# A diffusion layer on one core: modulation weights in a ring of half tiles, the latent rows loaded through another queue

## The chip, the cores and the metric

The kernel runs on one core of one Trainium2 chip. The metric is device time in microseconds (us) for one execution of the whole layer. The engines are named as the profile names them: PE (matrix products) with PEld (its weight loads), DVE (vector), ACT (scalar functions), POOL (GpSimd), and SP, which here issues most of the DMAs. Each engine runs its own instructions strictly in order. A DMA is issued from the instruction queue of SP or POOL, so an issue that has to wait for a free buffer holds up whatever stands behind it on that queue.

## The reference, cut to what matters

```
m       = silu(cond) @ w_mod + b_mod            # 6 vectors: shift, scale, gate for two norms; 2 conditions
h       = rms_norm(x) * g * (1 + scale1) + shift1
q,k,v,xr,yg = split(h @ w_in)
o       = concat(window_attention(q,k,v,sink), rglru(conv(xr)) * gelu(yg)) @ w_out
x1      = x + gate1 * o
h2      = rms_norm(x1) * g * (1 + scale2) + shift2
y       = x1 + gate2 * PEER(h2)                 # 8 heads, top 16 of 128x128 product keys, 16384 experts
out     = rms_norm(y) * g_final
```

There are 256 context tokens, which read only context, and 1024 latent tokens, which read their window and all the context keys; the latent recurrence starts from given states. All of it is float32. A product of two float32 matrices is done as three products of their high and low parts.

## The kernel before

A tile is 128 tokens: there are 2 context tiles and 8 latent ones. The stages, with the names that the profile's rows carry:

1. **Modulation** (`modulations`, L156). `w_mod` is 24 MB, in 3 parts of 8 blocks. Each block is one DMA of 1 MB into a tile `w` of 8 KB per partition, in a ring of 6 (48 KB per partition), and feeds 4 products (L190) that add into a PSUM tile `p`, of which there are two. Part 0 gives `a1` and `b1`, the scale and shift of the first norm. The function then yields; parts 1 and 2, of use from the output projection on, are written after the context attention but may be placed anywhere earlier.
2. **Context first norm and projection** (`project`, L258). For each tile: sum of squares on ACT (L277), `rstd_of` (a power on POOL, L147, small DVE steps), scaling on DVE (L279), 8 transposes on PE (L248) whose results DVE (L253) and ACT (L255) scale and shift, and a split into high and low parts `hh` (ACT, L134) and `hl` (DVE, L135). Then 14 column blocks of `w_in` (load L286, split `wh` on ACT, `wl` on DVE, 24 products each), with the recurrence `recur` between them.
3. **Context attention**, scores L424, exponentials L439; **context finish** (`finish`, `w_out` loads L501, products L526); **context choice** of experts (`choose`, `combine`).
4. **Latent**: the same `project`, with the rows of `x_sample` loaded by SP (L272) into two buffers `x`, with two buffers `f`; then recurrence, rotary turns on POOL (L333), attention, finish, choice.
5. **Spread** (L697 to L709): one-hot products that write the weights of the chosen experts as a dense matrix for 6 latent tiles. Early experts (products `u`, L1028) run beside it. **Dense** experts from about 1703 us to the end.
6. **Gathers**: the other 4 tiles (2 context, 2 latent) fetch each chosen expert's two rows by indirect DMAs on POOL (L859 for `peer_u`, L873 for `peer_v`), one DVE instruction each (L862, L879). They are 4 x 128 rows of either kind. A counter (`tick`) issues them a few at a time between the other work, from the context choice on; those of the context tiles are 512 DVE instructions with their gathers, the first 249 of which stand ahead of the dense stage.

What sets the order: a list scheduler takes the instructions by priority (the order in which they are written, with `tick`'s insertions) as soon as its own model finds the inputs ready and a buffer free, and so fixes the order on each engine before the program runs. SBUF pools are stacked from either end. A pool that opens after others have closed takes their addresses and then has to wait for their last readers. The latent first norm's `x` and `f` tiles lay on addresses of the modulation pool and so came after the last L190.

## Time and profile before

| | |
|---|---|
| median of 3 runs | 3565.87 us (3563.97 to 3566.43) |
| profiled execution | 3568.34 us |
| its span | 3566.5 us |
| mean granted clock of PE | 0.955 of full speed |
| busy: PE, DVE, ACT, POOL | 90%, 87%, 40%, 48% of the span |
| chain that ended last | PE 43%, DVE 22%, issue 8%, DMA 8% |

The shares of busy time are means over stages that have different limits. The rows further down therefore cut the span into ten stretches, whose borders are: 41.5 us, the first split `wh` of the context projection; 128.9 us, the first exponential of the context attention; 173.4 us, its last output; 252.2 us, the context choice; 482.6 us, the first rotary product; 690 us, the latent finish; 885 us, the latent choice; 1230 us, the spread; 1619.4 us, the last product of the spread; 1703 us, the dense stage. An engine whose busy time nearly fills a stretch limits it there; where none does, a chain of waits or a DMA does.

### The profile page before, as it was taken

To read this page: it belongs to the slowest core of one execution; us is meant where nothing else is said; L and a number is where in the kernel's file an instruction comes from. 1 tells how busy PE (TensorE), PEld (TensorE's weight loads), DVE (VectorE), ACT (ScalarE), POOL (GpSimd) and SP (SyncE) were. 2 spreads that over 40 slices of the span, in tenths; PEclk is the share of its full clock that TensorE was granted. 3 is DMA by queue.
4 is the path that set the end of the run, shared out by engine and by line. 5 is a ranking of instruction groups with operands and counts; after the bars stand their busy time and mean duration, and the time that the engine had idled before them with its cause. 6 is when DMAs were issued, how large, how long until landed. Compare 5 with 4: busy or idle time off the path is not lost.

```text
span 3566.5 us, 48580 instructions
## 1 busy us (share of the span) xinstructions
PE 3210.4 (90%) x16982; PEld 2704.1 (76%) x16982; DVE 3111.0 (87%) x6762; ACT 1429.9 (40%) x2242; POOL 1716.4 (48%) x1146
## 2 busy tenths in 40 slices
PE   7788868777999888888899999999999999999994
PEld 4477645433889877778788888878888887888884
DVE  4649989877999999993599999989999998999998
ACT  5734647523112344433333334333334333333432
POOL 0012451466521223443266666656666655666665
PEclk9799989988999999999999999999999999999997
DMA  8342652588621367795699999989999998999996
GB/s 331 136 152 82 216 206 83 185 276 290 219 89 31 122 199 214 233 315 185 242 325 337 337 330 334 340 308 335 329 328 339 327 340 290 332 327 336 335 339 223
DMA packets 349141, 918.19 MB, mean 257 GB/s; under 512 B 29144, under 2 KB 150104, under 8 KB 345824
## 3 DMA queue, kind: packets, MB, share of 16 engines
q0 software_dynamic: 147456, 536.94, 42.9%
q1 hardware_dynamic: 201440, 378.16, 30.8%
q8 instruction: 133, 2.18, 0.2%
q14 instruction: 112, 0.92, 0.1%
HBM read 834.48 MB, written 80.50 MB: 257 GB/s over the span
## 4 chain that ended last, share of the span: by engine, by line
PE 43%; DVE 22%; issue 8%; DMA 8%; POOL 3%; ACT 2%; SPq 0%; POOLq 0%; DVEq 0%; ACTq 0%
PE u L138 6%; PE u L140 6%; PE u L139 6%; PE rot L138 5%; PE rot L140 5%; PE rot L139 5%; DVE acc L879 3%; DVE row L862 3%; DMA row<-in_peer_u,eid 2%; PE res L138 2%; PE res L139 2%; PE res L140 2%; DMA row<-in_peer_v,eid 2%; DMA ad<-a 2%; DVE oh L699 1%
## 5 line engine op out<-in xcount | busy, mean ns | idle before, releaser
L859 POOL DMA_INDIRECT row<-in_peer_u,eid x512 | 749.9, 1465 | 603.3 <-DVE acc L879 201.7
L873 POOL DMA_INDIRECT row<-in_peer_v,eid x512 | 719.9, 1406 | 583.6 <-DVE acc L879 283.7
L138 PE MATMUL u<-hh,uh 128*128 128x384 f32 x2048 | 707.1, 345 | 22.4 <-ACT a L1028 22.4
L140 PE MATMUL u<-hh,ul 128*128 128x384 f32 x2048 | 705.6, 345 | 4.7 <-DVE ul L135 4.7
L139 PE MATMUL u<-hl,uh 128*128 128x384 f32 x2048 | 707.1, 345 | 0.0
L879 DVE SCALAR_TENSOR_TENSOR acc<-row,w,acc 128x1024 f32<-128x1024 f32 x508 | 663.4, 1306 | 25.2 <-DMA row<-in_peer_v,eid 23.7
L862 DVE SCALAR_TENSOR_TENSOR row<-row,h 128x1024 f32<-128x1024 f32 x512 | 623.0, 1232 | 62.8 <-DMA row<-in_peer_u,eid 62.6
L764 ACT ACTIVATE q<-rot 128x512 f32<-128x512 f32 x504 | 300.0, 597 | 523.5 <-PE rot L140 295.5
L138 PE MATMUL rot<-vh,ah 128*128 128x512 f32 x1024 | 409.1, 400 | 16.6 <-ACT q L764 16.1
L138 PEld LDWEIGHTS u<-hh,uh 128*128 128x128 f32 x2048 | 394.7, 193 | 29.8 <-ACT a L1028 23.8
L140 PEld LDWEIGHTS u<-hh,ul 128*128 128x128 f32 x2048 | 394.2, 192 | 9.7 <-DVE ul L135 5.1
L139 PE MATMUL rot<-vl,ah 128*128 128x512 f32 x1024 | 401.4, 392 | 0.0
L140 PE MATMUL rot<-vh,al 128*128 128x512 f32 x1024 | 400.6, 392 | 0.0
L139 PEld LDWEIGHTS u<-hl,uh 128*128 128x128 f32 x2048 | 394.6, 193 | 4.5
L765 DVE TENSOR_TENSOR acc<-q,acc 128x512 f32<-128x512 f32 x504 | 341.8, 686 | 45.4 <-ACT q L764 42.3
L140 PE MATMUL mm<-hh,wl 128*128 128x256 f32 (+2 forms) x848 | 289.7, 342 | 9.8 <-POOL wl L135 6.9
L138 PE MATMUL mm<-hh,wh 128*128 128x256 f32 (+2 forms) x848 | 286.3, 338 | 5.6 <-ACT wh L134 5.6
L139 PE MATMUL mm<-hl,wh 128*128 128x256 f32 (+2 forms) x848 | 284.3, 335 | 0.0
L134 ACT ACTIVATE uh<-u 128x1024 fp32r<-128x1024 f32 x128 | 135.8, 1061 | 331.3 <-PE u L139 302.0
L135 POOL TENSOR_TENSOR ul<-u,uh 128x1024 fp32r<-128x1024 f32 x44 | 122.8, 2791 | 277.8 <-ACT uh L134 237.5
L138 PEld LDWEIGHTS rot<-vh,ah 128*128 128x128 f32 x1024 | 193.4, 189 | 74.9 <-ACT q L764 36.7
L140 PEld LDWEIGHTS rot<-vh,al 128*128 128x128 f32 x1024 | 193.2, 189 | 41.5
(271 smaller groups left out, 5955.3 us busy)
## 6 DMA issues: line engine op xcount, KB each, us to landing
u<-in_ut SPq DMA_DIRECT2D x128, 512.0 KB
v<-in_peer_v SPq DMA_DIRECT2D x128, 512.0 KB
gd<-stg SPq DMA_DIRECT2D x12, 4096.0 KB
gt<-gd SPq DMA_DIRECT2D x64, 768.0 KB
w<-in_w_mod SPq DMA_DIRECT2D x24, 1024.0 KB
ad<-a SPq DMA_DIRECT2D x88, 192.0 KB
a<-ad SPq DMA_DIRECT2D x44, 384.0 KB
w<-in_w_query SPq DMA_DIRECT2D x32, 512.0 KB
```

The lines of the kernel that those rows point to most:

```text
L134: A.activation(hi, src, AF.Copy)
L135: return (eng or V).tensor_tensor(lo, src, hi, op=OP.subtract)
L138: T.matmul(out, lhs[0], rhs[0], start=first, stop=False)
L139: T.matmul(out, lhs[0], rhs[1], start=False, stop=False)
L140: T.matmul(out, lhs[1], rhs[0], start=False, stop=last)
L699: V.tensor_tensor(oh.rearrange(four, j=2), o2.rearrange(four, j=2), pairs(gh, ts), op=OP.mult)
L764: A.activation(q, p, AF.Copy)
L765: tick(share / (2 * (N_DENSE - N_RES)), V.tensor_tensor(y, q, y, op=OP.add))
L859: G.indirect_dma_start(out=u, out_offset=None, in_=i["peer_u"], in_offset=bass.IndirectOffsetOnAxis(ap=eid[:, k:k + 1], axis=0))
L862: V.scalar_tensor_tensor(u, u, 1.0, h2, op0=OP.mult, op1=OP.mult, accum_out=act[:, j:j + 1])
L873: G.indirect_dma_start(out=v, out_offset=None, in_=i["peer_v"], in_offset=bass.IndirectOffsetOnAxis(ap=eid[:, k:k + 1], axis=0))
L879: V.scalar_tensor_tensor(acc, v, w[:, j:j + 1], acc, op0=OP.mult, op1=OP.add)
```

## The change

One PSUM tile `p` instead of two. Each block of `w_mod` comes as two DMAs of 0.5 MB into tiles of 4 KB per partition, in a ring of 4 such halves (16 KB per partition). The latent first norm's pool is no longer stacked on the modulation pool. Its rows are loaded from POOL's queue. Lines after L179 are numbered one higher in the changed kernel.

```diff
--- before.py
+++ after.py
@@ -173,10 +173,11 @@
         bmod = p1.tile([P, 3, 512], F32, name="bmod")
         modr = p1.tile([P, 3, 512], F32, name="modr")
         for n in range(3):
-            p = ps.tile([P, 512], F32, name="p", bufs=2)
+            p = ps.tile([P, 512], F32, name="p")
             for k in range(KD):
-                w = p1.tile([P, 4, 512], F32, name="w", bufs=6)
-                nc.sync.dma_start(w, i["w_mod"][n, k])
+                ws = [p1.tile([P, 2, 512], F32, name="w", bufs=4) for _ in range(2)]
+                for h, w in enumerate(ws):
+                    nc.sync.dma_start(w, i["w_mod"][n, k, :, 2 * h:2 * h + 2])
                 if n == 0 and k in (2, 3):
                     u = len(xc)
                     xc.append(p1.tile([P, D], F32, name=f"x{u}"))
@@ -187,7 +188,7 @@
                     gffn = load("gffn", [P, KD])
                     nc.sync.dma_start(bmod, i["bmod"])
                 for j in range(4):
-                    T.matmul(p[32 * j:32 * j + 32], sig[:, k], w[:, j], start=(k == 0), stop=(k == KD - 1),
+                    T.matmul(p[32 * j:32 * j + 32], sig[:, k], ws[j // 2][:, j % 2], start=(k == 0), stop=(k == KD - 1),
                              tile_position=(0, 32 * j), skip_group_check=True)
             V.tensor_tensor(modr[:, n], p, bmod[:, n], op=OP.add)
             pc = ps.tile([P, 4, P], F32, name="pc")
@@ -269,7 +270,7 @@
                 us = slice(u * P, (u + 1) * P)
                 if lat:
                     x = xp.tile([P, D], F32, name="x", bufs=2)
-                    nc.sync.dma_start(x, x_in[us, :])
+                    G.dma_start(x, x_in[us, :])
                 else:
                     x = xc[u]
                 f = xp.tile([P, KD, P], F32, name="f", bufs=2)
```

The scheduler's order changes with it up to the start of the dense stage; from there on the order is the same on every engine. Three places:

**SP from the context attention to the context finish.** `x_sample` are the latent rows, `w_out` the weights of the output projection, `w_in` here those of the latent input projection. Before:

```order
L272 DMA x<-in_x_sample 128x1024 x2
L319 DMA out_new_k<-kk 128x2x128
L207 DMA modd<-modr 2x512 x2
L272 DMA x<-in_x_sample 128x1024
L929 DMA out_new_rnn<-ends 128x8
L350 DMA wg<-in_w_rg 128x256 x2
L272 DMA x<-in_x_sample 128x1024 x5
L501 DMA w<-in_w_out 128x256 x8
```

After:

```order
L320 DMA out_new_k<-kk 128x2x128
L208 DMA modd<-modr 2x512 x2
L930 DMA out_new_rnn<-ends 128x8
L351 DMA wg<-in_w_rg 128x256 x2
L287 DMA w<-in_w_in 128x1024 x3
L502 DMA w<-in_w_out 128x256 x8
L212 DMA ga_1422<-modd 128x1024
L518 DMA x<-in_x_prompt 128x1024 x2
L287 DMA w<-in_w_in 128x1024
```

The eight loads of latent rows have left SP's queue. The first `w_out` loads stood behind five of them; now three latent `w_in` loads stand ahead. All eight row loads are now on POOL's queue, two at its very start and six between the powers L147.

**ACT at the start of the context attention.** `f<-tr` and `hh` belong to the latent first norm, `f,ss` is its sum of squares, `pr` are the exponentials. Before:

```order
L255 ACTIVATE f<-tr,b_89,a_88 128x128
L370 ACT_TABLE_LOAD
L370 ACTIVATE bv_877<-bv_877 128x256
L439 ACT_TABLE_LOAD
L439 ACTIVATE pr,sums<-s,negm 128x256 x2
L255 ACTIVATE f<-tr,b_89,a_88 128x128 x2
L134 ACTIVATE hh<-f 128x8x128
L439 ACTIVATE pr,sums<-s,negm 128x256 x2
L443 ACTIVATE den<-den 128x4
L277 ACTIVATE f,ss<-x 128x1024
L450 ACTIVATE pr<-pr,den 128x256 x4
L439 ACTIVATE pr,sums<-s,negm 128x256 x2
```

After:

```order
L256 ACTIVATE f<-tr,b_89,a_88 128x128
L371 ACT_TABLE_LOAD
L371 ACTIVATE bv_893<-bv_893 128x256
L440 ACT_TABLE_LOAD
L440 ACTIVATE pr,sums<-s,negm 128x256 x2
L256 ACTIVATE f<-tr,b_89,a_88 128x128
L134 ACTIVATE hh<-f 128x8x128
L440 ACTIVATE pr,sums<-s,negm 128x256 x2
L444 ACTIVATE den<-den 128x4
L451 ACTIVATE pr<-pr,den 128x256 x4
L440 ACTIVATE pr,sums<-s,negm 128x256 x2
L470 ACTIVATE pT<-pt 128x512
```

The norm of the latent tiles stood among the exponentials. It now stands ahead of them: three of its sums of squares and four of its transposes' copies come before the first `wh` of the context projection, and between that and the first exponential ACT has 5 sums of squares (2 before), 11 L255 (1) and 6 `hh` (0).

**POOL and DVE where the gathers stand.** On POOL, from the last power of the norm to the first rotary products `kT` and `qT`. Before:

```order
L147 TENSOR_TENSOR rs_r<-rs_m,nhalf 128x1 x12
L135 TENSOR_TENSOR wl<-w,wh 128x1024 x16
L859 DMA row<-in_peer_u,eid_2156 128x1024 x16
L873 DMA row<-in_peer_v,eid_2156 128x1024 x16
L859 DMA row<-in_peer_u,eid_2156 128x1024 x11
L333 TENSOR_TENSOR kT<-kT,cosT 128x512
L859 DMA row<-in_peer_u,eid_2156 128x1024
L333 TENSOR_TENSOR kT<-kT,cosT 128x512
L333 TENSOR_TENSOR qT<-qT,cosT 128x512 x6
```

After:

```order
L147 TENSOR_TENSOR rs_r<-rs_m,nhalf 128x1 x4
L135 TENSOR_TENSOR wl<-w,wh 128x1024 x16
L860 DMA row<-in_peer_u,eid_2204 128x1024 x16
L874 DMA row<-in_peer_v,eid_2204 128x1024 x16
L860 DMA row<-in_peer_u,eid_2204 128x1024 x16
L874 DMA row<-in_peer_v,eid_2204 128x1024 x7
L334 TENSOR_TENSOR kT<-kT,cosT 128x512
L874 DMA row<-in_peer_v,eid_2204 128x1024
L334 TENSOR_TENSOR kT<-kT,cosT 128x512
L334 TENSOR_TENSOR qT<-qT,cosT 128x512 x6
```

Sixteen `peer_u` gathers and then sixteen `peer_v` gathers make a block. 55 gathers are issued ahead of the first rotary product where there were 43; 12 more DVE row instructions (52, were 40) stand ahead of it too. Counted the same way, the number of row instructions done before a point rises by 16 at the first latent score, 18 at the last, 18 at the first latent norm of the finish, 23 at the last split there, 22 at the last choice and 26 at the first step of the spread, and is the same, 249, after the last step: 39 stood within the spread, now 13.

On DVE at the end of the spread (`oh` are its one-hot matrices; L613, L614 after the change, begins the last `combine`). Before:

```order
L697 TENSOR_TENSOR oh_13001<-iota,tw_12615 128x1024
L700 TENSOR_TENSOR oh_12977<-oh_12977,tw_12618 128x1024
L698 TENSOR_TENSOR oh_13002<-iota,tw_12616 128x1024
L879 SCALAR_TENSOR_TENSOR acc<-row,w,acc 128x1024
L699 TENSOR_TENSOR oh_13003<-oh_13002,tw_12617 128x1024
L613 TENSOR_TENSOR key<-idxs_6676 128x4x16
L700 TENSOR_TENSOR oh_13002<-oh_13002,tw_12618 128x1024
L613 TENSOR_TENSOR cand<-vals_6675 128x4x8
```

After:

```order
L701 TENSOR_TENSOR oh_13000<-oh_13000,tw_12666 128x1024
L699 TENSOR_TENSOR oh_13025<-iota,tw_12664 128x1024
L700 TENSOR_TENSOR oh_13026<-oh_13025,tw_12665 128x1024
L698 TENSOR_TENSOR oh_13049<-iota,tw_12663 128x1024
L701 TENSOR_TENSOR oh_13025<-oh_13025,tw_12666 128x1024
L699 TENSOR_TENSOR oh_13050<-iota,tw_12664 128x1024
L700 TENSOR_TENSOR oh_13051<-oh_13050,tw_12665 128x1024
L701 TENSOR_TENSOR oh_13050<-oh_13050,tw_12666 128x1024
L135 TENSOR_TENSOR vl<-v,vh 128x1024
```

The last `combine` came after the spread's last one-hot matrices; it now ends among them. On PE the early experts' products `u` within the spread fall from 1220 to 1152, 48 of them being one step of an early expert.

## Rows read from the trace of the kernel before

**Rows 1.** Stretches: length, busy us of PE, PEld, DVE, ACT, POOL, clock, DMA, GB/s

```profile
0.00:41.50 41.50, 21.06 (x108) 5.94 (x108) 13.09 (x56) 9.32 (x17) 1.29 (x6) 0.92 0.95 368
41.50:128.90 87.40, 75.19 (x500) 55.12 (x500) 48.81 (x99) 69.13 (x103) 1.60 (x2) 0.95 0.71 257
128.90:173.40 44.50, 33.86 (x112) 18.50 (x112) 32.06 (x102) 33.78 (x88) 2.70 (x5) 0.65 0.20 58
173.40:252.20 78.80, 67.38 (x306) 53.09 (x307) 29.73 (x58) 31.15 (x53) 6.53 (x6) 0.96 0.49 158
252.20:482.60 230.40, 202.60 (x996) 157.67 (x994) 211.09 (x729) 128.20 (x164) 95.98 (x56) 0.98 0.49 159
482.60:690.00 207.40, 157.07 (x863) 99.01 (x865) 180.36 (x361) 121.31 (x268) 67.29 (x56) 0.90 0.41 134
690.00:885.00 195.00, 141.49 (x389) 67.00 (x387) 138.39 (x200) 58.97 (x113) 121.58 (x96) 0.87 0.84 284
885.00:1230.00 345.00, 313.65 (x1882) 302.13 (x1881) 335.85 (x1972) 81.28 (x133) 108.51 (x68) 0.94 0.38 120
1230.00:1619.40 389.40, 341.50 (x2783) 301.39 (x2781) 368.32 (x801) 169.66 (x206) 134.74 (x64) 0.95 0.76 233
1619.40:1703.00 83.60, 73.81 (x417) 73.17 (x414) 24.69 (x166) 22.88 (x34) 21.51 (x12) 0.96 0.50 160
```

**Rows 2.** DMA packets in 63-67, 15-20 and 155-162 us

```profile
DMA packets 221, 1.68 MB, mean 420 GB/s; under 512 B 16, under 2 KB 16, under 8 KB 16
...
DMA packets 352, 2.09 MB, mean 418 GB/s; under 512 B 33, under 2 KB 33, under 8 KB 161
...
DMA packets 144, 0.52 MB, mean 75 GB/s; under 512 B 16, under 2 KB 16, under 8 KB 144
q1 hardware_dynamic: 144, 0.52, 23.1%
```

**Rows 3.** SP's issues in order: start, length, line, tensor, count

```profile
29.28 1.33 SPq L179 DMA_DIRECT2D w<-in_w_mod  x3
30.66 1.49 SPq L286 DMA_DIRECT2D w<-in_w_in  x2
...
132.70 38.95 SPq L272 DMA_DIRECT2D x<-in_x_sample  x5
```

**Rows 4.** PE in order: start, length, line, count, idle before and releaser

```profile
34.19 1.97 PE L248 MATMUL tr<-ident,x 128*128 128x128 f32 x8 [2.31 <-ACT f L255]
42.61 0.39 PE L138 MATMUL mm<-hh,wh 128*128 128x256 f32 x1 [1.71 <-ACT wh L134]
```

**Rows 5.** ACT by line and shape, 103-203 us: busy, mean ns | idle

```profile
L134 ACT ACTIVATE hh<-f 128x1024 fp32r<-128x1024 f32 x8 | 8.4, 1055 | 0.1
L277 ACT ACTIVATE f<-x 128x1024 f32<-128x1024 f32 x8 | 8.4, 1053 | 4.7 <-DVE hl L135 4.7
L255 ACT ACTIVATE f<-tr,b,a 128x128 f32<-128x128 f32 x16 | 7.1, 456 | 21.1 <-DVE f L253 20.4 <-DVE ends L382 0.7
```

**Rows 6.** DVE by line and shape, 253 to 482 us

```profile
L371 DVE SCALAR_TENSOR_TENSOR gi<-gi,xc 128x1024 f32<-128x1024 f32 x8 | 9.8, 1220 | 0.2 <-ACT gi L359 0.2
L375 DVE TENSOR_TENSOR_SCAN bv<-av,chan,gi 128x1024 f32<-128x1024 f32 x4 | 9.4, 2346 | 0.0
```

**Rows 7.** DVE by line, 690 to 885 us: busy, mean ns | idle, releaser

```profile
L879 DVE SCALAR_TENSOR_TENSOR acc<-row,w,acc 128x1024 f32<-128x1024 f32 x44 | 56.5, 1284 | 22.1 <-DMA row<-in_peer_v,eid 21.4
L862 DVE SCALAR_TENSOR_TENSOR row<-row,h 128x1024 f32<-128x1024 f32 x42 | 53.0, 1269 | 27.4 <-DMA row<-in_peer_u,eid 27.2
```

**Rows 8.** The same, 1230 to 1620 us, the spread

```profile
L879 DVE SCALAR_TENSOR_TENSOR acc<-row,w,acc 128x1024 f32<-128x1024 f32 x23 | 35.6, 1547 | 0.0
L862 DVE SCALAR_TENSOR_TENSOR row<-row,h 128x1024 f32<-128x1024 f32 x16 | 21.6, 1351 | 0.0
```

**Rows 9.** The columns of rows 1, while the last choice is combined

```profile
1616.40:1640.00 23.60, 16.73 (x107) 16.10 (x105) 21.82 (x133) 10.39 (x14) 6.75 (x4) 0.96 0.91 276
```

**Rows 10.** ACT in order of time: start, length, line [idle, releaser]

```profile
1636.64 1.28 ACT L627 ACT_TABLE_LOAD   x1 [9.05 <-DVE nm L626]
```

## Prediction

> **What bounds the kernel now.** I read the busy time by stretch first. Up to 41.5 us DMA is at 0.95 and 368 GB/s, so the front is bound by the loads of `w_mod`; in the context projection PE has 75.2 of 87.4 us and ACT 69.1; in the context attention no engine has over 33.9 of 44.5 us and the granted clock is 0.65, so a chain through DVE, ACT and PE bounds it; from the context choice to the rotary turns DVE has 211.1 and PE 202.6 of 230.4; the latent finish is again filled by none; in the spread DVE has 368.3 of 389.4 [rows 1]. After the spread DVE is busy 24.7 of 83.6 us, and PE, with the early experts, is the bound [rows 1]. The busiest rows of the latent finish give its bound: DVE waits 21.4 + 27.2 us for gathered rows in 195 us [rows 7]. I then read the order of SP, since a wait there is unseen in busy times: five loads of latent rows take SP from 132.70 us for 38.95 us, with `w_out` behind them [rows 3]. The order from the dense stage on is unchanged, so the time changes by as much as the start of that stage, at 1703 us, moves. The sum is made against the profiled execution, 3568.3 us (span 3566.5 and 1.8 around it), which is 2.5 above the median of the runs; the result is put back on the median.
>
> **The front, +7.** The order puts 16 more transposes on PE and 6.6 us of the norm on ACT here, both idle for half of it or more [rows 1]: free. Three things cost. First, three latent row tiles, 1.5 MB, load here: at 420 GB/s, the full rate [rows 2], 3.6 us, against one block of `w_mod` less (22 halves, 11 MB, ahead of the first `w_in` load, where 12 MB were), 2.4 us: net +1.2. Second, packets halve to 4 KB. Of the 221 packets in 63 to 67 us 205 are of 8 KB, of the 352 in 15 to 20 us 191 are and 128 are of 4 KB, and both run at 418 to 420 GB/s [rows 2]: by these the halving is free. In a lone row load 128 packets of 4 KB took 23.1% of 16 engines for 7 us, at most 202 ns each, where 205 of 8 KB in 4 us are 312 each [rows 2]: two for one would be 29% dearer, or 7.6 us on the 26 us that 11 MB take at 420 GB/s. I take nearer the free end, since those packets were under load as here: +1. Third, the ring. SP issued three blocks at 29.28 and the first two `w_in` at 30.66 [rows 3], before the second context tile's transposes at 34.19 [rows 4]. With four halves, half 22 needs half 18 read, and on PE half 18 stands behind those transposes, which end at 36.2 us. So `w_in` is issued at about 37 to 38, and four halves and its own 0.5 MB behind that, 2.6 MB at 420 GB/s, are 6 us: the first `wh` at 44 us or later, where it was 41.5; with the two items above 46 to 50. I take 48.5. Bounds +1 (the ring's wait falls beside loads that queue in any case) and +14 (dear packets on top).
>
> The Trainium skill ("DMA: Bandwidth & Descriptors", section "Measured (HBM→SBUF, 128 partitions, SWDGE, issued from GpSimd)") asks for DMAs of at least 1 MiB to reach 75% of the peak, which speaks against halving these, and gives one DMA as 2.0 us and its bytes at 436 GB/s (section "Anatomy of one DMA — SWDGE (gpsimd) path"): an estimate of 3.2 us for a half, 70 us for 22 halves if nothing overlapped, and a sum of some +50. The 418 GB/s at 15 to 20 us, with 0.5 MB loads among the blocks, bear out the row instead, so the rule changes no term here; no row shows a stretch of halves alone.
>
> **Context projection, +8.** By the order ACT gets 3 more L277 at 1.24 us (with the read-out of 0.19), 10 L255 at 0.456 and 6 `hh` at 1.055 [rows 5]: 3.7 + 4.6 + 6.3 = 14.6 us on 69.1 of 87.4 [rows 1]. ACT's 18.3 idle us could cover it all (0), or none of it (+14.6); PE, 75.2 busy, gets 37 transposes more at 0.25 us (8 in 1.97 [rows 4]), 9 us, and it too has 12 idle. ACT feeds PE here through `wh`, so half is covered: +8. The ring's wait on PE, two halves of slack in place of five blocks, sits in the same range.
>
> **Context attention, -12.** 6 L277, 14 L255 and 7 `hh` leave ACT: 7.4 + 6.4 + 7.4 = 21.2 us [rows 5], and 53 transposes leave PE, 13 us; in come 61 latent projection products, 12 us at 0.20 (202.6 us for 996 [rows 1]), and their splits. ACT, at 33.8 of 44.5 [rows 1], falls to some 24. The chain of scores, exponentials and outputs that is left is known only by its parts; 28 to 40 us, I take 32.5. The `w_out` loads, no longer behind five row loads [rows 3], start with it.
>
> **Context finish, +4.** It takes 35 more latent products, 7 us on PE at 67.4 of 78.8 [rows 1], and the first latent recurrence begins earlier; what it costs lies between 0 and 8.
>
> **Choice to rotary turns, -4.** 12 more row instructions at 1.28 us: +15.4. The first block of the latent recurrence has left: two scans of 2.35 and two gate products of 1.22 [rows 6], with two further products of each direction of about that size, 12.5 us. DVE would be +3; PE is relieved of 96 products, some 20 of its 202.6 us. DVE has 19.3 us idle, part of it waiting on PE: between +3 and -12.
>
> **Rotary turns to the end of the latent attention, +8:** 6 rows more at 1.28, in stretches where DVE is the fullest at 180.4 of 207.4 [rows 1]. **Latent finish, +10.** 44 + 42 rows pass in 195 us, 2.27 each, waiting for the gather [rows 7]. Five more cost 11, if the gather is the bound through it; if they fit beside it, 6. **Latent choice, +4:** the balance then reaches 26 after 3 more rows, 1.3 each.
>
> **Spread, -14.** 39 rows took 35.6 + 21.6 us, 1.47 each [rows 8]. 26 fewer: -38. The last `combine`, 21.8 busy us in 23.6 where PE's tail hid it [rows 9], moves in: +22. The early products on PE fall by 68, at 0.177 us a product (73.8 us for 417 [rows 1]) 12 us, and 2 us of DVE's waits on PE go with them.
>
> **After the spread, -1.** ACT waited 9.05 us for `nm` of that `combine` [rows 10], and the early experts' activation stood behind it; that goes. One step of an early expert, 48 products of 0.177, 8.5 us, comes after the spread in its place.
>
> The sum: 7 + 8 - 12 + 4 - 4 + 8 + 10 + 4 - 14 - 1 = **+10**, or 3578 on the profiled execution and **3576 us** against the median.
>
> **Rivals.**
> 1. *Faster: the rows fit into idle DVE time.* The 26 rows that leave the spread give back 38 us there whatever happens ahead. DVE idles 19 us from the choice to the rotary turns, 27 to the end of the attention, 57 in the latent finish [rows 1]. If the rows land in that time, those stretches cost -9, +3, +3 and +1 instead of -4, +8, +10 and +4: -20 on the sum, some 3556, and 3546 if rival 3 holds as well. For it: the idle time is four times what 26 rows need. Against it: in the finish the idle time is itself a wait for rows. It decides if the choice to the spread, 252.2 to 1230, takes under 978 us as it did, with 22 rows more.
> 2. *Slower by much: the small ring starves the projection.* Each `w_in` load stands on SP behind halves of `w_mod` that wait for PE to read four halves back, and PE reads them in order between the projection's products, which wait for `w_in`. Every such round would show the 6 us of the front again; there are 14 column blocks, and six of them with halves ahead of them make +25 on the projection in place of 8, some 3595 to 3604. For it: DMA was at 0.71 there even with the long ring. Against it: `w_in` has two buffers of its own. It decides from a first exponential later than 150 us.
> 3. *Nothing: the early norm is covered.* ACT idles 18 us of the projection and 32 of the front [rows 1]; the latent norm's steps fit in, `w_in` is issued no later than now, and front and projection together cost +4 instead of +15: 3565, no change. For it: the idle time exceeds the 14.6 us of work. Against it: ACT stands in the chain from `w_in` to PE, so what is put ahead of a `wh` delays it though ACT idles later. It decides if the first exponential comes by 134 us.
>
> **How the numbers follow.** The forecast, slower by some us, has 0.42; rival 1 0.26; rival 2 0.12; rival 3 0.20. 0.2%, about what a measurement can tell from no change, is 7 us: below 3558.7 faster, above 3573.0 slower. Of the forecast's 0.42, 0.04 falls under that mark; rival 3 is all within it. Faster 0.26, same 0.24, slower 0.50. The forecast's own range, from its bounds, is 3564 to 3592. With the rivals the range is 3547 to 3603, which leaves the far ends of rivals 1 and 2 out.
>
> **What would show each step.** First `wh` of the context projection at 46 to 50 us, with `w_in` issued by SP after 36; first exponential at 140 to 147; attention of 28 to 36 us, ending at 172 to 180; the choice starting at 255 to 266; DVE's waits for rows in the latent finish of 50 us or more; a spread of 370 to 380 us, with hardly any row in it and the `combine` among its last steps; no wait of ACT on `nm` after it; the dense stage at about 1713. The forecast fails if the first `wh` comes by 43 us, if the attention doesn't shrink, or if the choice to the spread takes the extra rows without growing.

## The result and the profile after

The changed kernel takes 3590.59 us (median of 3, 3588.82 to 3593.03) against 3565.87: ratio 1.0071, 95% interval 1.0048 to 1.0094, 24.7 us slower. The forecast was 3576, range 3547 to 3603: the sign was right, the size was 10 in place of 25. The profiled execution took 3593.03 us, its span 3591.1.

Ten instructions, each the first or the last of its kind, mark off the stages in both traces. Each time is the start of such an instruction, in us, so a difference is the length of a stage. The stages of the sum are read against them:

| stage, from and to | before | after | change | forecast |
|---|---|---|---|---|
| front, to the first `wh` (41.5; 52.9) | 41.5 | 52.9 | +11.4 | +7 |
| projection, to the first exponential (128.9; 152.9) | 87.4 | 100.1 | +12.6 | +8 |
| attention, to its last output (172.9; 190.7) | 44.0 | 37.8 | -6.2 | -12 |
| finish, to the context choice (253.4; 268.7) | 80.5 | 78.0 | -2.5 | +4 |
| choice, to the rotary turns (482.6; 505.2) | 229.2 | 236.6 | +7.3 | -4 |
| rotary turns and latent attention (676.6; 704.2) | 194.0 | 199.0 | +5.0 | +8 |
| latent finish, to its last product with `qT` (855.0; 884.5) | 178.4 | 180.3 | +1.9 | +10 |
| latent choice, to the spread (1222.5; 1255.5) | 367.5 | 371.0 | +3.5 | +4 |
| spread, to its last product (1619.3; 1644.1) | 396.8 | 388.6 | -8.3 | -14 |
| to the first dense `rot` (1717.3; 1746.7) | 98.0 | 102.6 | +4.6 | -1 |
| dense, to the end | 1849.2 | 1844.4 | -4.8 | 0 |

The busy times of some of these stretches, with the columns of [rows 1]: the projection, the attention, the latent finish and the spread of the changed kernel.

```profile
52.90:152.90 100.00, 85.83 (x536) 60.54 (x536) 69.99 (x156) 82.70 (x127) 5.40 (x10) 0.93 0.69 236
152.90:191.20 38.30, 36.12 (x129) 21.84 (x130) 15.00 (x49) 25.62 (x70) 0.00 (x0) 0.77 0.15 49
704.20:884.50 180.30, 142.11 (x393) 65.54 (x392) 133.48 (x208) 53.35 (x103) 111.35 (x89) 0.91 0.83 282
1255.50:1644.10 388.60, 337.45 (x2750) 296.78 (x2749) 363.34 (x977) 175.95 (x213) 101.77 (x40) 0.95 0.67 200
```

As forecast, ACT is fuller in the projection, 82.7 us where it had 69.1 in [rows 1], and the spread is shorter, with less work for DVE. The dense stage, forecast at no change, took 4.8 us less; in the fourteen profiled executions of this document it takes from 1843.0 to 1850.1 us, so I read nothing into it.

**The front.** What answers to [rows 3] and [rows 4]: SP's issues, with what SP waited for from 37 to 46.3 us; then PE and ACT in order of time.

```profile
30.42 0.42 SPq L82 DMA_DIRECT2D chan<-in_chan  x1
37.24 9.09 SPq L180 DMA_DIRECT2D w<-in_w_mod  x6
46.39 0.90 SPq L287 DMA_DIRECT2D w<-in_w_in  x2
SPq L180 <- PE p L191: 4.4, 2, 4.2
SPq L180 <- DMA w<-in_w_mod: 2.3, 1, 2.3
...
38.69 0.66 PE L196 MATMUL pc<-ident,modr 128*128 128x128 f32 x4 [0.79 <-DVE modr L193]
53.97 0.38 PE L138 MATMUL mm<-hh,wh 128*128 128x256 f32 x1 [1.80 <-ACT wh L134]
...
46.83 1.06 ACT L134 ACTIVATE hh<-f 128x1024 fp32r<-128x1024 f32 x1
48.27 1.06 ACT L134 ACTIVATE hh<-f 128x1024 fp32r<-128x1024 f32 x1
50.86 1.06 ACT L278 ACTIVATE f<-x 128x1024 f32<-128x1024 f32 x1 [1.53 <-DVE hl L135]
52.87 1.04 ACT L134 ACTIVATE wh<-w 128x1024 fp32r<-128x1024 f32 x1
```

Part 0 of the modulation ends with the transposes at 38.69 (30.76 before). SP needs 9.09 us for six halves, of which it waits 4.4 for PE to read a half and 2.3 for a half to land, and the first `w_in` load is issued at 46.39, where [rows 3] has 30.66. It lands 6.2 us later, at 52.6. On ACT an `hh` (48.27) and a sum of squares of the latent norm stand ahead of the first `wh`, the sum waiting 1.53 us for DVE's `hl`; the `hh` at 46.83 is the second context tile's. So two things are late at the same time, and experiments have to tell which one counts.

**From the choice to the first latent score.** The busy times before, and the waits of DVE in that stretch (instruction, what it waited for: us in total, times, longest), before and after:

```profile
253.40:533.90 280.50, 228.02 (x1077) 174.13 (x1075) 248.85 (x780) 142.23 (x193) 122.69 (x76) 0.94 0.50 168
DVE vals L588 <- PE sc L585: 14.3, 7, 6.4
DVE row L862 <- DMA row<-in_peer_u,eid: 7.3, 5, 3.4
DVE acc L879 <- DMA row<-in_peer_v,eid: 1.3, 1, 1.3
...
DVE row L863 <- DMA row<-in_peer_u,eid: 13.4, 12, 3.3
DVE acc L880 <- DMA row<-in_peer_v,eid: 7.5, 12, 1.2
DVE row L863 <- issue: 4.2, 1, 4.2
```

The wait for PE's scores has gone, 14.3 us, as I had expected of a PE relieved of latent products. In its place DVE waits for gathered rows, 20.9 us where it waited 8.6. DVE is busy 260.3 us of 292.0 (the row stands with e5 below), and was 248.9 of 280.5: it is idle 31.7 us in both, and the stretch grew by what DVE has more to do, 11.4 us.

**Latent finish and spread.** What answers to [rows 7]; then the spread before; then the busy times from the spread's start to the dense stage, before and after; then ACT behind the spread, after.

```profile
L863 DVE SCALAR_TENSOR_TENSOR row<-row,h 128x1024 f32<-128x1024 f32 x48 | 58.5, 1223 | 27.8 <-DMA row<-in_peer_u,eid 27.4
L880 DVE SCALAR_TENSOR_TENSOR acc<-row,w,acc 128x1024 f32<-128x1024 f32 x36 | 46.2, 1283 | 14.1 <-DMA row<-in_peer_v,eid 13.7
...
1222.50:1619.30 396.80, 348.90 (x2817) 308.79 (x2816) 375.72 (x846) 172.87 (x210) 138.28 (x67) 0.95 0.76 232
...
1222.50:1717.30 494.80, 427.87 (x3245) 385.80 (x3244) 407.78 (x1018) 200.50 (x249) 159.89 (x78) 0.94 0.72 223
1255.50:1746.70 491.20, 424.80 (x3224) 382.04 (x3223) 370.96 (x985) 199.32 (x247) 123.75 (x51) 0.94 0.65 195
...
1662.17 1.13 ACT L1029 ACTIVATE a<-u 128x384 f32<-128x384 f32 x2 [11.25 <-DMA ad<-a]
```

From the spread's start to the dense stage DVE has 36.8 us less to do, 371.0 for 407.8, and the stretch is only 3.6 us shorter. But 24.4 of the 36.8 left the stretch behind the spread, where DVE had been busy 32.1 of 98.0 us. In the spread itself DVE has 12.4 less, 363.3 for 375.7, and the spread is 8.3 shorter. Over the eleven kernels that don't hold the rows back by hand (e8 to e10 do) the spread takes 370 to 400 us with 354 to 376 us of DVE's work in it, so DVE is busy for 93 to 97% of it in each.

Behind the spread ACT's wait of 9.05 us for `nm` [rows 10] is gone, as forecast. In its place ACT waits 11.25 us until the store of an early expert's activations (`ad`) has landed, while the DMA share from 1652 to 1662 us is 1.05. Before, that share was already 0.91 [rows 9].

### The profile page after: what moved, and what is told of

Read it like the earlier page. It is cut to its first block, busy times and chain, and to the rows that moved or that the text cites. A ratio compares the mean times of both kernels' runs of the same rounds, so it can differ in the third digit from the quotient of the medians.

```text
span 3591.1 us, 48646 instructions
## 1 busy us (share of the span) xinstructions
PE 3220.1 (90%) x16982; PEld 2700.2 (75%) x16982; DVE 3102.5 (86%) x6762; ACT 1431.4 (40%) x2244; POOL 1714.6 (48%) x1154
## 3 DMA queue, kind: packets, MB, share of 16 engines
q0 software_dynamic: 148608, 541.13, 42.9%
## 4 chain that ended last, share of the span: by engine, by line
PE 39%; DVE 11%; issue 6%; DMA 4%; POOL 2%; ACT 1%; SPq 0%; POOLq 0%; DVEq 0%; ACTq 0%
PE u L139 6%; PE u L138 6%; PE u L140 6%; PE rot L138 4%; PE rot L140 4%; PE rot L139 4%; PE res L138 2%; PE res L140 2%; PE res L139 2%; DVE acc L880 2%; DVE row L863 2%; DMA row<-in_peer_u,eid 1%; DVE oh L700 1%; DVE acc L766 1%; DMA a<-ad 1%
## 5 line engine op out<-in xcount | busy, mean ns | idle before, releaser
L860 POOL DMA_INDIRECT row<-in_peer_u,eid x512 | 736.3, 1438 | 615.7 <-DVE acc L880 211.0
L138 PE MATMUL u<-hh,uh 128*128 128x384 f32 x2048 | 705.4, 344 | 10.9 <-ACT a L1029 10.9
L138 PEld LDWEIGHTS u<-hh,uh 128*128 128x128 f32 x2048 | 392.7, 192 | 20.9 <-ACT a L1029 11.7
L135 DVE TENSOR_TENSOR vl<-v,vh 128x1024 fp32r<-128x1024 f32 x128 | 155.7, 1217 | 98.3 <-DMA gt<-gd 94.4
```

The lines of the kernel that those rows point to most:

```text
L135: return (eng or V).tensor_tensor(lo, src, hi, op=OP.subtract)
L138: T.matmul(out, lhs[0], rhs[0], start=first, stop=False)
L860: G.indirect_dma_start(out=u, out_offset=None, in_=i["peer_u"], in_offset=bass.IndirectOffsetOnAxis(ap=eid[:, k:k + 1], axis=0))
```

## The experiments

All twelve side by side: starts in the profiled execution of each, in us (part 0 is the add that ends it, `exp` the first exponential, score the first latent score, dense the first `rot`); how many row instructions stand ahead of the first latent score and of the spread, and how many latent projection products ahead of the choice, by the order; and the ratio to the kernel before, from all runs, with its interval. "Norm early" says whether most of the latent first norm stands ahead of the first exponential.

| kernel | part 0 | `w_in` | `wh` | exp | choice | score | spread | dense | rows | products | norm early | ratio |
|---|---|---|---|---|---|---|---|---|---|---|---|---|
| before | 30.0 | 30.7 | 41.5 | 128.9 | 253.4 | 533.9 | 1222.5 | 1717.3 | 48, 210 | 100 | no | 1 |
| changed | 37.9 | 46.4 | 52.9 | 152.9 | 268.7 | 560.7 | 1255.5 | 1746.7 | 64, 236 | 156 | yes | 1.0071 (1.0048, 1.0094) |
| e1 | 37.5 | 44.8 | 51.2 | 140.3 | 271.1 | 554.2 | 1240.9 | 1739.4 | 48, 210 | 100 | no | 1.0059 (1.0030, 1.0087) |
| e2 | 31.8 | 33.7 | 42.9 | 137.3 | 256.3 | 537.6 | 1222.0 | 1717.9 | 48, 210 | 100 | no | 1.0023 (1.0010, 1.0035) |
| e3 | 35.2 | 37.8 | 49.0 | 138.6 | 265.2 | 566.3 | 1264.2 | 1754.7 | 64, 236 | 125 | no | 1.0093 (1.0064, 1.0123) |
| e4 | 37.5 | 50.4 | 60.2 | 160.8 | 281.7 | 546.5 | 1242.3 | 1723.2 | 47, 220 | 192 | yes | 1.0028 (1.0014, 1.0043) |
| e5 | 36.6 | 45.0 | 56.0 | 154.1 | 270.9 | 539.2 | 1230.4 | 1722.2 | 48, 210 | 183 | yes | 1.0020 (1.0004, 1.0037) |
| e6 | 35.8 | 43.7 | 49.0 | 142.3 | 267.3 | 576.0 | 1275.6 | 1760.6 | 62, 233 | 96 | no | 1.0119 (1.0084, 1.0155) |
| e7 | 32.7 | 33.4 | 44.8 | 133.2 | 257.6 | 577.8 | 1273.9 | 1755.1 | 74, 242 | 105 | no | 1.0120 (1.0084, 1.0156) |
| e8 | 37.9 | 46.0 | 52.5 | 151.6 | 267.2 | 541.6 | 1241.5 | 1731.8 | 40, 210 | 156 | yes | 1.0087 (1.0072, 1.0103) |
| e9 | 30.2 | 30.8 | 42.1 | 129.8 | 253.8 | 527.6 | 1216.5 | 1726.3 | 32, 205 | 100 | no | 1.0056 (1.0043, 1.0069) |
| e10 | 36.7 | 45.2 | 56.1 | 153.9 | 271.3 | 529.7 | 1228.8 | 1743.3 | 32, 205 | 183 | yes | 1.0074 (1.0061, 1.0086) |
| e11 | 38.9 | 37.3 | 53.2 | 150.7 | 266.5 | 558.7 | 1253.6 | 1743.3 | 64, 236 | 156 | yes | 1.0082 (1.0068, 1.0096) |
| e12 | 36.8 | 35.4 | 53.2 | 154.0 | 271.0 | 541.6 | 1256.4 | 1740.9 | 47, 220 | 166 | yes | 1.0036 (1.0023, 1.0049) |

Single executions of one kernel spread by some 10 to 13 us to either side, so the ratios decide on totals. The profiled execution of e8 was 13.6 us below the median of its runs, that of e2 9.4 below, of e9 5.7 below, and of e12 10.7 above; the others lie within 5 us of theirs. Three pairs differ by their edits only behind the choice (the kernel before and e9, the changed one and e8, e5 and e10): their times are 0.1 to 0.6 us apart at the first `wh` and 0.4 to 1.5 at the choice, so smaller differences there say nothing.

**e1: the ring without the early norm.** Theory A: the small ring. Theory B: the norm's steps.

```diff
-            p = ps.tile([P, 512], F32, name="p")
+            p = ps.tile([P, 512], F32, name="p", bufs=2)
```

> The changed kernel with two PSUM tiles p again; ring of 4 halves and row loads on POOL stay. By its order the latent norm goes back among the context attention's exponentials (8 of its sums of squares and all its hh splits behind the first one) and the gathers stand as in the kernel before (40 row instructions ahead of the rotary turns). So it has the small ring and two early row loads without the early norm. Theory A (the small ring delays w_in and the projection): first wh at 50 to 53 us as in the changed kernel (52.9; 41.5 before), first exponential at 145 to 150, the end 15 to 20 us above the kernel before, 3581 to 3586. Theory B (the norm's steps, put ahead of wh and between the projection's products, cause the delay): first wh at 42 to 45, first exponential at 129 to 134, 3566 to 3572.

With the second PSUM tile the norm and the rows are back about where they were before; two of the eight latent sums of squares still run in the front. The first `wh` is late all the same. SP and ACT in order of time:

```profile
44.77 1.48 SPq L287 DMA_DIRECT2D w<-in_w_in  x2
...
51.22 1.06 ACT L134 ACTIVATE wh<-w 128x1024 fp32r<-128x1024 f32 x1 [5.68 <-DMA w<-in_w_in]
```

`wh` waits 5.68 us for its load: here the loads are what is late, not the norm. The choice is 17.7 us late and the end 21 by the ratio. A holds for the first `wh` and the end; the first exponential, 140.3, came earlier than A has it. The early norm, the difference between the changed kernel and e1 at the choice, is worth 2.4 us: it costs 1.7 at the first `wh` and 10.9 in the projection, and returns 13.0 in the attention and 2.0 in the finish.

**e2: the halving alone, in a deep ring** (with one tile `p`, as in the changed kernel).

```diff
-                w = p1.tile([P, 4, 512], F32, name="w", bufs=6)
+                ws = [p1.tile([P, 2, 512], F32, name="w", bufs=12) for _ in range(2)]
```

> The kernel before with each block of w_mod loaded as two halves, ring of 12 halves (48 KB per partition as before), one PSUM tile p, row loads on SP: the halving of packets alone, with the norm and the gathers in the order of before. Theory A (depth of the ring, not packet size): first wh at 41 to 44 us, total within 4 us of 3566. Theory C (4 KB packets and twice the issues are dearer): first wh at 46 to 50, DMA share near 0.95 up to it, total 3571 to 3578.

```profile
15.00:20.00 5.00, 3.21 (x12) 0.36 (x9) 1.49 (x5) 1.15 (x2) 0.55 (x1) 0.76 1.03 411
20.00:25.00 5.00, 4.76 (x24) 1.38 (x24) 1.49 (x5) 1.15 (x2) 0.56 (x1) 1.00 1.03 410
```

The last two columns are DMA share and GB/s: 410 GB/s with nothing but halves. Part 0 is 1.8 us later, the choice 2.9, the total 0.23%, some 8 us, though its profiled execution shows no loss from the choice on. Theory A is right on the first `wh`, 42.9, and its total, within 4 us, was missed by some 5. Halving is nearly free in the front. The rule of 1 MiB in the Trainium skill ("DMA: Bandwidth & Descriptors", section "Measured (HBM→SBUF, 128 partitions, SWDGE, issued from GpSimd)") doesn't decide here: 410 GB/s is 94% of the 436 which that page has for the peak.

**e3: the changed kernel with twelve halves.**

```diff
-                ws = [p1.tile([P, 2, 512], F32, name="w", bufs=4) for _ in range(2)]
+                ws = [p1.tile([P, 2, 512], F32, name="w", bufs=12) for _ in range(2)]
```

> The changed kernel with 12 halves in the ring in place of 4. By its order 52 row instructions stand ahead of the rotary turns as in the changed kernel and the combine is within the spread, but most of the latent norm is again behind the first exponential (6 of 8 sums of squares). Theory A: first wh at 42 to 46, first exponential at 130 to 136, and about 15 to 20 us of the 24.7 come back: 3570 to 3576; what stays above 3566 is the choice to the first latent score (292 us in the changed kernel, 280.6 before), given back in the spread. Theory B: the projection also comes back to 88 to 92 us, as the norm has left it, but the first wh would stay at 50 or later since the loads on POOL stay.

A did not come: with a deep ring the first `wh` is at 49.0, and the total is the worst of the first four, with 301.1 us from the choice to the score. Of B the projection came, 89.6 us, and the first `wh` missed its mark by 1 us. The norm is late here, the rows are where the changed kernel has them. The edit differs from e2's in the row loads on POOL alone, which so cost 6.1 us at the first `wh` and 8.9 at the choice.

**e4: two whole blocks.**

```diff
-                w = p1.tile([P, 4, 512], F32, name="w", bufs=6)
+                w = p1.tile([P, 4, 512], F32, name="w", bufs=2)
```

and one tile `p` and POOL's loads, as in the changed kernel.

> A ring of two whole 1 MB blocks: the same 16 KB per partition as the changed kernel's four halves, with packets of 8 KB. The norm is as early as in the changed kernel (4 latent sums of squares ahead of the first wh, 4 between it and the first exponential). 34 row instructions ahead of the rotary turns. Theory A: as late or later than the changed kernel, first wh at 53 to 62 us, since a load can start only when a whole block has been read. Theory C: first wh at 43 to 48, as packets are 8 KB again. Total by A 3590 to 3605, by C 3570 to 3580.

A was right on the front, 60.2 us, and wrong on the total: 28.3 us late at the choice, and only 0.28%, some 10 us, at the end. The total is in theory C's range, but C's first `wh`, 43 to 48, did not come. So lateness at the choice is not lateness at the end. 192 latent products are done by then, where before had 100.

**e5: the first two row loads behind part 0.**

```diff
+                    if u < 2:
+                        G.tensor_copy(x[:, 0:2], b1[:, 0, :])
                     G.dma_start(x, x_in[us, :])
```

> The changed kernel, but the first two latent rows' tiles are first touched by a small POOL copy that reads b1, so their loads can't be issued before part 0 of the modulation is done. Ring of 4 halves and early norm stay. By its order 38 row instructions stand ahead of the rotary turns and 210 ahead of the spread (52 and 236 in the changed kernel; 40 and 210 before). Theory A (front: the early row loads take 3 to 6 us from the modulation loads, the ring holds w_in back by the rest): part 0 done at 34 to 35.5 us (37.9 in the changed kernel, 31.8 with deep halves), first wh at 48 to 51 (52.9). Theory G (the gathers' place costs some 6 us net): from the choice to the spread 975 to 982 us (986.8), the spread 396 to 400 (388.6), total 3576 to 3584. If neither, 3588 to 3592.

Part 0 comes 1.3 us earlier, the first `wh` 3.1 later, and the choice no earlier than in the changed kernel, yet the end is at 0.20%, some 7 us: 18 us of the 25 are back. They come back between the choice and the score. Busy times and the waits for rows there:

```profile
270.90:539.20 268.30, 210.31 (x965) 159.95 (x964) 240.74 (x774) 123.44 (x172) 129.80 (x76) 0.89 0.51 169
DVE row L865 <- DMA row<-in_peer_u,eid: 9.1, 8, 2.5
DVE acc L882 <- DMA row<-in_peer_v,eid: 0.6, 1, 0.6
DVE vals L591 <- PE sc L588: 13.4, 7, 8.4
...
268.70:560.70 292.00, 213.40 (x995) 163.45 (x993) 260.27 (x791) 126.41 (x175) 140.13 (x92) 0.89 0.55 184
```

DVE has 19.5 us less to do there than in the changed kernel (240.7 for 260.3), and it waits 9.7 us for rows, not 20.9; the stretch is 23.7 us shorter. Neither theory has these numbers: A's first `wh`, 48 to 51, came at 56.0, and from the choice to the spread it took 959.5 us, where G has 975 to 982. The wait for PE's scores is 13.4 us here, though PE has done more latent products early than in the changed kernel; so that PE was relieved of them doesn't by itself explain why this wait is gone there.

**e6 and e7: the ring alone, POOL's loads alone.** e6 is e1 with the rows loaded by SP; e7 is the kernel before with

```diff
-                    nc.sync.dma_start(x, x_in[us, :])
+                    G.dma_start(x, x_in[us, :])
```

> Ring of 4 halves and two PSUM tiles p, the latent rows loaded from SP: the ring alone, without early row loads and without early norm (8 of 8 sums of squares behind the first exponential; 48 row instructions ahead of the rotary turns). Theory A with the ring as the main cost: part 0 done at 34 to 36 us, w_in issued at 42 or later, first wh at 48 to 51, the choice at 265 to 270. If the early row loads of POOL are the main cost instead (theory L): part 0 at 32 to 33, first wh at 43 to 46, the choice at 256 to 260.

> The kernel before with the row loads on POOL's queue and nothing else: ring of six 1 MB blocks. Two row tiles load at the start; 60 row instructions stand ahead of the rotary turns and 242 ahead of the spread by its order. Theory A: part 0 at 32 to 34 us (30.0 before), first wh at 43 to 46 (41.5), the choice at 254 to 259 (253.4). Theory L: first wh at 47 to 50, the choice at 262 to 268. Theory G (gathers ahead of the rotary turns cost their DVE time): the choice to the first latent score grows by 18 to 26 us from 280.5, and the spread shrinks by 5 to 15 from 396.8.

At the choice e6 is 13.9 us late and e7 4.2, which makes 18.1, where e1, which has both, is 17.7 late: here the two add up. Theory A has the front of both right, in every number. Of e6's 13.9 the halving is 2.9 (e2), so the depth is some 11, with two tiles `p` in e6 and one in e2. These prices hang on what they are added to: in the deep ring of halves the loads on POOL cost 8.9 (e3 against e2), and the depth then costs 5.9 (e1 against e3). In e7 two row tiles put part 0 off by 2.7 us; 1 MB at the 420 GB/s of [rows 2] is 2.5. That is what the Trainium skill says in "DMA: Bandwidth & Descriptors", section "Issuing engines are not separate DMA queues": a load from another engine's queue still shares the same 16 DMA engines. Both kernels are slowest of all at the end, by 1.2%, and what makes them so comes after the choice: 308.7 and 320.2 us to the score. e7's waits for rows there:

```profile
DVE row L862 <- DMA row<-in_peer_u,eid: 17.8, 16, 2.5
DVE acc L879 <- DMA row<-in_peer_v,eid: 6.3, 6, 1.9
DVE row L862 <- issue: 5.2, 1, 5.2
```

Theory G has the direction for e7 and not the size: +39.7 to the score, where 18 to 26 were expected, and -26.9 in the spread for 5 to 15. Over all kernels without a hold the stretch from the choice to the score takes 265 to 283 us with 47 or 48 rows in it, 292 to 309 with 62 to 64, and 320 with 74.

**e8, e9, e10: the rows held by hand.** An order-only edge on DVE:

```diff
+        held[0] += 1
+        return tc.issue_after(held[1]) if held[1] is not None and held[0] > 40 else nullcontext()
```

with `held[1]` the first subtraction of the latent attention; 40 in e8, on the changed kernel; 32 in e9, on the kernel before, and in e10, on e5.

> The changed kernel with an order-only edge: from the 41st gathered row on, a row's DVE instruction is queued behind the first subtraction of the latent attention. Ring, loads and early norm are untouched up to the choice. 40 row instructions stand ahead of the first latent score (64 in the changed kernel, 48 before), 210 ahead of the spread (236; 210). Theory G (what moved the time is the place of the rows; the front's loss is returned by latent work done early): the choice starts at 268.7 as in the changed kernel, from there to the first latent score 256 to 264 us (292.0), 24 rows at 1.2 to 1.5 each, total 3563 to 3573. Theory A (the front's 15 us are what the end is late by): the choice to the spread falls but the spread and what follows grow by as much, total 3584 to 3592.

> The kernel before with the same edge from the 33rd row on: 32 row instructions ahead of the first latent score (48), 205 ahead of the spread (210). Theory G: the choice to the first latent score shrinks from 280.5 by 16 rows at 1.2 to 1.5, to 256 to 262; some comes back in the finish and the spread, total 3548 to 3562. If rows only change places at an even price: within 4 us of the kernel before.

> The kernel of e5_late_rows (small ring, early norm, first row loads after part 0) with the edge from the 33rd row on: 32 ahead of the first latent score (48 there), 205 ahead of the spread (210). Theory G: the choice to the first latent score at 244 to 252 us (268.3 there), total 3550 to 3562. At an even price: 3566 to 3572 as there.

In each the stretch to the score is shorter, by 17.6, 6.7 and 9.9 us; none is faster at the end, and theory G's stretches and totals are missed in all three. e8 stays at the ratio of the changed kernel, e9 loses 20 us against its own base and e10 19. The rows cost 0.4 to 0.7 us each where they were taken away, less than the 1.28 that a row instruction takes, so they had filled idle time: DVE's idle time in the stretch grew by 10 to 13 us. Put off, they cost more. In e9, from the spread's start to the dense stage:

```profile
1216.50:1726.30 509.80, 429.44 (x3219) 385.69 (x3218) 402.80 (x1031) 203.82 (x252) 181.52 (x82) 0.93 0.70 220
DVE oh L704 <- PE g L708: 40.6, 16, 6.0
...
DVE oh L699 <- PE g L703: 18.9, 15, 4.4
```

DVE's wait for PE in the spread doubles, 40.6 us for 18.9, with only five rows more in it. Theory G, that the rows' place alone is the loss, is refuted as far as totals go.

**e11 and e12: `w_in` first.** On the changed kernel and on e5:

```diff
-                    nc.sync.dma_start(w, i["w_mod"][n, k, :, 2 * h:2 * h + 2])
+                    with tc.issue_after(wins[1]) if n >= 1 and True else nullcontext():
+                        nc.sync.dma_start(w, i["w_mod"][n, k, :, 2 * h:2 * h + 2])
```

with `wins` the `w_in` loads of the context projection.

> The changed kernel with an order-only edge on SP: the loads of parts 1 and 2 of the modulation are queued behind the first two w_in loads, so these no longer stand behind halves that wait for PE. The norm stays as early, and the gathers stand as in the changed kernel (64 row instructions ahead of the first latent score, 236 ahead of the spread). Theory A (the ring holds w_in back, and what is late at the choice is late at the end): w_in issued at 36 to 39 us (46.4 in the changed kernel), first wh at 45 to 49 (52.9), the choice at 261 to 266 (268.7), total 3580 to 3587. Theory S (what the front loses is taken up later, as in e5_late_rows): choice as by A, but the dense stage within 3 us of the changed kernel's, total 3587 to 3593.

> The kernel of e5_late_rows with the edge of e11_w_in_first: small ring, early norm, first row loads after part 0, the first two w_in loads ahead of parts 1 and 2. 47 row instructions ahead of the first latent score, 220 ahead of the spread. Theory A: first wh at 46 to 50 us (56.0 in e5_late_rows), the choice at 262 to 266 (270.9), total 3554 to 3563, a little faster than the kernel before. If the rows' place decides more than the front (10 more rows ahead of the spread than there): 3566 to 3575.

```profile
37.29 0.91 SPq L289 DMA_DIRECT2D w<-in_w_in  x2
...
49.24 1.06 ACT L135 ACTIVATE hh<-f 128x1024 fp32r<-128x1024 f32 x1
51.82 1.06 ACT L280 ACTIVATE f<-x 128x1024 f32<-128x1024 f32 x1 [1.53 <-DVE hl L136]
53.22 1.04 ACT L135 ACTIVATE wh<-w 128x1024 fp32r<-128x1024 f32 x1
...
54.32 0.58 PE L139 MATMUL mm<-hh,wh 128*128 128x256 f32 x1 [3.94 <-ACT wh L135]
```

In e11 `w_in` is issued 9.1 us earlier than in the changed kernel, and the first `wh` comes at 53.2, where it was 52.9: it now has its data (no DMA moves anything from 45.5 to 50 us) and waits for its turn on ACT, behind an `hh` and a sum of squares of the latent norm. Nothing is gained at the first `wh` or at the end; the choice comes 2.2 us earlier. The total, 3592.6, is in theory S's range. Theory A's step for the front falls: in the changed kernel the late load and the norm hold the first `wh` to about the same time, and taking away either (e1, e11) returns at most 1.7 us of 11.4. e12 is no better than e5: its first `wh` at 53.2, its choice at 271.0 and its total of 3579.46 are outside both theories.

No kernel here beats the one before; e5, the nearest, is 0.20% slower (0.04 to 0.37).

## Why the prediction was right in sign and short in size

**Front, +7 forecast, +11.4 measured.** The packets at +1 were right (e2: 1.4 at the first `wh`). The early loads were netted to +1.2; e7 shows 3.3 at the first `wh`. The ring's hold on `w_in` was found, with an issue at 37 to 38 us, and it came at 46.39. What was missing is that the ring also holds the halves of part 0: part 0 ends 7.9 us later, and with the ring and no early loads (e6) 5.8 later, of which the halving is 1.8 (e2). The loads and the ring without the early norm make +9.7 (e1). The sentence that the norm's 16 transposes and 6.6 us on ACT were free, since the engines were idle half the time, failed too, if for at most 1.7 us here. ACT is idle there, but in order: e11 shows `wh` behind the norm's steps with its load at hand. The price was to be read from what stands between, not from the idle time.

**Projection and attention.** Half of ACT's added work was charged, +8, and +12.6 came; against e1, which has the same ring and loads, the early norm costs 10.9 there for its 14.6 of work. The attention gave back half of the forecast, -6.2 for -12: it ended at 190.7, after the forecast of 172 to 180. The sum of these and the finish, what the early norm itself does behind the front, was forecast at 0 and is -4.1 against e1. That part of the argument holds, with both sides mis-sized. So the choice is 15.3 us late, where +7 was forecast: 17.7 for the loads and the ring (halving 2.9, early row loads 4, depth of the ring 11, in the order in which e2, e7 and e6 add them), less 2.4 for the early norm.

**Choice to rotary turns, -4 forecast, +7.3 measured.** This step failed most, and not in the work: DVE's busy time grew by 3.4 us (214.4 for 211.0), +3 was forecast, and PE's fell by 13.0 (188.4 for 201.4), 20 was forecast. PE's relief did come, and the wait for its scores went, 14.3 us to 0.7; I let that count against DVE's idle time. But the idle time did not shrink, 22.1 us for 18.2, since DVE's waits for gathered rows grew in the same stretch from 3.1 to 15.0 us, with 4.2 more before one row for which the profile shows no cause. Busy times with the columns of [rows 1] and DVE's waits for rows from the choice to the rotary turns, before and after:

```profile
253.40:482.60 229.20, 201.40 (x988) 156.67 (x986) 211.04 (x729) 127.85 (x163) 95.98 (x56) 0.98 0.49 159
DVE row L862 <- DMA row<-in_peer_u,eid: 1.8, 2, 1.4
DVE acc L879 <- DMA row<-in_peer_v,eid: 1.3, 1, 1.3
...
268.70:505.20 236.50, 188.40 (x916) 147.56 (x914) 214.40 (x743) 110.05 (x143) 109.93 (x68) 0.92 0.53 174
DVE row L863 <- DMA row<-in_peer_u,eid: 11.5, 11, 3.3
DVE row L863 <- issue: 4.2, 1, 4.2
DVE acc L880 <- DMA row<-in_peer_v,eid: 3.5, 6, 1.1
```

I had applied the price of a gather-bound row only to the finish, where [rows 7] shows it; there the stretch grew by 1.9 us and not 10, and DVE waited 41.1 us for rows, where 50 or more were to show.

**Rotary turns to the dense stage, +7 forecast, +6.7 measured.** The total is right by offsets: finish too dear by 8, attention by 3, spread too kind by 6, what follows it too kind by 6. The spread was priced by DVE's work, and by its own terms (-38, +22, -2) the price is -18, not the -14 that stands in the sum. Measured, DVE's work there fell by 12.4 us, and its idle time grew from 21.1 to 25.3, so 8.3 came. Behind the spread the stretch is 4.6 us longer, where -1 was forecast. The 48 products `u` that were charged do stand there (462 for 414, PE 81.9 us for 73.9). The step that failed is the credit of 9.05 us for the wait on `nm`: the wait for the store of `ad`, 1.34 us behind it before, took its place with 11.25.

**The rivals.** Rival 1, rows in idle DVE time, decided by the choice to the spread (my cut, 252.2 to 1230, is nearest to the choice and the spread's start here): 969.1 to 986.8, longer by 17.7, so it did not happen. (The idle time held in its favour, 103 us, is three times the 33 us that 26 rows need at 1.28, not four.) Rival 3, the covered norm: the first exponential came at 152.9, not by 134. Rival 2, the starved projection, was to show from a first exponential later than 150 us; it was later, but by the norm: without it (e1) the projection takes 89.1 us, near the 87.4 of before. Its mark did not tell it from the forecast.

**Luck.** The total lies just within the forecast's own range, 3564 to 3592, though the first `wh`, the first exponential, the attention and the choice all lie outside the marks named for them. The ten steps miss by -8 to +11 us each, some 37 us in all one way and 18 the other.

**What stays open.** e5 has the changed kernel's ring, its early norm and its lateness at the choice, and is 18 us faster. Two things differ behind the choice: 16 rows fewer ahead of the score, whose 20.5 us are about what DVE has less to do there, and 183 latent products done by the choice in place of 156. For the rows: in the eleven kernels without a hold DVE's work from the choice to the score goes from 236 to 284 us, its idle time only from 26 to 36, so the stretch is as long as DVE's work makes it. Against it: e8 held the rows by hand and gained nothing by its median; there DVE stood idle for 44.6 us of the stretch to the score, 27.6 in e5, so a hold by hand is not the place that the scheduler found. That the products alone do it was not tried, nor what is between executions of e8, 24 us from fastest to slowest. What is shown is where the 18 us lie and that DVE has as much less to do there, not which of the two differences brings them.

## What to carry to other kernels

An engine that is half idle still delays what stands behind the added work in its order: before calling moved work free, name the next instruction that somebody waits for, and count what now stands ahead of it. An engine's idle time is no store to be filled: from the choice to the score DVE was idle for 26 to 36 us, whether 47 rows stood there or 74. A ring that is just deep enough by bytes isn't by order, if the issuing queue is shared: its waits for the consumer hold up every other load there. A wait that goes gives back only the time to the next wait behind it (9.05 us for `nm`, then 11.25 for a store). And a small change of pools can move work in far stages through the scheduler, here 26 gathered rows, so the order there is to be priced as carefully as the edit itself, and tested with an edge that fixes the order while the edit stays.

## What was not expected of the hardware

Halving 1 MB loads to packets of 4 KB cost 1.8 us on 30 in a stretch bound by DMA (e2), at 410 GB/s in place of 418 to 421. And executions of one kernel differ more than the first three showed: those of the kernel before, 3563.97 to 3566.43 there, ran from 3553.04 to 3578.93 in twenty later ones, so that a difference of 7 us between two single profiles says nothing here.
